# The second MLP product of a decoder layer, by Strassen's scheme for 24 of its 32 feature blocks

## The chip, the cores and the metric

The kernel runs on one NeuronCore of a Trainium2 chip. Five engines work side by side, each through its own queue in order: TensorE (PE) multiplies matrices into PSUM, VectorE (DVE) and ScalarE (ACT) work on SBUF and PSUM elementwise, GpSimd (POOL) on SBUF only, and SyncE (SP) issues transfers. Transfers can be issued from SP, ACT and POOL, and run on 16 DMA engines. The metric is the device time of one execution in microseconds (us).

## The reference

One layer on x of shape 512 x 1024 in float32: an input LayerNorm, a token mixer (gated linear attention beside multi-head latent attention), a LayerNorm over the residual, then the MLP and a last LayerNorm. The change touches the MLP alone:

```python
h = layer_norm(x, ln_in_g, ln_in_b)
mix = token_mixer(h, ...)
h = layer_norm(DEEPNORM_ALPHA * h + mix, ln1_g[l], ln1_b[l])
ff = jnp.square(jax.nn.relu(h @ w_ff1[l])) @ w_ff2[l]
h = layer_norm(DEEPNORM_ALPHA * h + ff, ln2_g[l], ln2_b[l])
```

`w_ff1` is 1024 x 4096 and `w_ff2` 4096 x 1024, all float32. The hidden width 4096 is 32 feature blocks of 128.

## The kernel before

**Precision.** Each float32 operand is held as two float32r parts: hi is the value copied by ACT into the float32r type, lo the rest, which DVE subtracts (`split`, and the same two instructions in `pump`). A product of two operands is three matmuls, hi x hi, hi x lo and lo x hi, added in one PSUM bank.

**The stream of weights.** All weight tiles of the whole kernel stand in one list, `stream`, in the order of their use. `plan` appends tiles of two row blocks by up to 512 columns. `pump(i)` runs ahead of tile i: it issues the loads from SP into `wraw` (three slots) two tiles ahead (`DMA_AHEAD`), and the split into `whi` and `wlo` (two slots each) one tile ahead (`SPLIT_AHEAD`). Tiles marked `res` get slots of their own in pool `pa` and may be split one further ahead.

**The products.** `gemm_fm` computes a product with features on the partitions: weights are stationary, 512 tokens move, and up to four PSUM banks are open. `gemm_tm` computes with tokens on the partitions: the activations are stationary (four tiles of 128 tokens), 512 weight columns move.

**The MLP.** It runs in chunks of 12, 12 and 8 feature blocks (`FC`, L321). For each chunk, the first product is computed with `gemm_fm` in groups of four blocks. `ev_h` (L1047) empties each bank: ACT relu, ACT square into hi of `hid`, POOL the full square, DVE the rest lo. The second product of a chunk then goes through `gemm_tm` for each half of the 1024 output columns, and `ev_res` (L980) adds each bank onto the residual tile `res` with DVE. For the last chunk the second product is ordered by token tiles, so that the last LayerNorm (`ln2`) and the stores can begin early.

**SBUF and PSUM.** Pool `pa` has a group A of 24 slots and a group C of 8 (`TAG_C`), 4 KB of each partition a slot; pool `pb` has 22 slots of 2 KB, of which the normalised input of the MLP, `h1T`, holds 16 until the last first product. The pools `pm` and `px` have four PSUM banks each.

**The order.** The program is written as generators that are stepped between matmuls (`spawn`, `tick`, `finish`). The framework then orders the instructions of each engine at build time, by the order in which they were written and by a simulated timeline, hands out the slots, and places the semaphores. `issue_after` asks for a place behind a given instruction.

Of the kernel before, what the change touches and what calls it, by code (L numbers as in the profile page):

```python
# [52 lines left out]
def tile_hybrid_block(ctx: ExitStack, tc: tile.TileContext, I, out, dbg=None):  # L53
    nc = tc.nc
    dbg = dbg or {}
    consts = ctx.enter_context(tc.tile_pool(name="consts", bufs=1))
    wp = ctx.enter_context(tc.tile_pool(name="wp", bufs=3))
    pa = ctx.enter_context(tc.tile_pool(name="pa", bufs=32))
    pb = ctx.enter_context(tc.tile_pool(name="pb", bufs=22))
    sm = ctx.enter_context(tc.tile_pool(name="sm", bufs=4))  # L60
# [5 lines left out]
    def nm(s):  # L66
        uid[0] += 1
        return f"{s}_{uid[0]}"

    TAG_C = ('h0', 'qn', 'PT1', 'res', 'bc', 'hid1')  # L70

    def A(shape, dt=F32, n="a"):
        return pa.tile(shape, dt, tag="C" if n in TAG_C else "A", bufs=8 if n in TAG_C else 24, name=nm(n))

    def B(shape, dt=F32, n="b"):
        return pb.tile(shape, dt, tag="B", name=nm(n))
# [26 lines left out]
    def split(src, hi, lo, scale=None):  # L103
        if scale is None:
            act(hi, src, AF.Copy)
            return vtt(lo, src, f(hi), op=ALU.subtract)
# [27 lines left out]
    st = {"dma": 0, "spl": 0, "gates": ()}  # L134
    DMA_AHEAD, SPLIT_AHEAD = 2, 1

    def plan(name, c0, n, k_lo=0, k_hi=None, heads=None, res=False):
        w = I[name]
        K = w.shape[0] // P
        k_hi = K if k_hi is None else k_hi  # L140
        idx = []
        for k0 in range(k_lo, k_hi, 2):
            nk = min(2, k_hi - k0)
# [10 lines left out]
        return {"idx": idx, "nk": k_hi - k_lo}  # L154

    def pump(i):
        while st["dma"] < min(len(stream), i + 1 + DMA_AHEAD):
            e = stream[st["dma"]]
            raw = wp.tile([P, 2, T], F32, tag="wraw", name=nm("wraw"))
            for sl, src, cw in e["dmas"]:  # L160
                dst = raw[:, sl, :e["n"]]
                if cw is not None:
                    dst = dst.rearrange("p (h c) -> p h c", c=cw)
                nc.sync.dma_start(dst, src)
            e["raw"] = raw
            st["dma"] += 1
        while st["spl"] < min(len(stream), i + 2 + SPLIT_AHEAD):
            e = stream[st["spl"]]
            if st["spl"] > i + SPLIT_AHEAD and not e["res"]:
                break  # L170
            nk, n = e["nk"], e["n"]
            if e["res"]:
                hi, lo = A([P, 2, T], F32R, "whr"), A([P, 2, T], F32R, "wlr")
            else:
                hi = wp.tile([P, 2, T], F32R, tag="whi", bufs=2, name=nm("whi"))
                lo = wp.tile([P, 2, T], F32R, tag="wlo", bufs=2, name=nm("wlo"))
            raw = e.pop("raw")
            with ExitStack() as gates:
                for g in st["gates"]:
                    gates.enter_context(tc.issue_after(g.ins))  # L180
                st["ins"] = act(hi[:, :nk, :n], raw[:, :nk, :n], AF.Copy)  # L181
                vtt(lo[:, :nk, :n], raw[:, :nk, :n], f(hi[:, :nk, :n]), op=ALU.subtract)  # L182
            st["gates"] = ()
            e["w"] = (hi, lo)
            st["spl"] += 1

    def weights(pl, k):
        i = pl["idx"][k // 2]
        pump(i)
        hi, lo = stream[i]["w"]  # L190
        return hi[:, k % 2, :], lo[:, k % 2, :]


    active = []
# [1 line left out]
    def spawn(g):  # L196
        active.append(g)
        return g
# [22 lines left out]
    def gemm_fm(pl, xs, n, evac, width=None, toks=slice(0, T), accs=None, guard=None):  # L221
        na = n // P
        accs = accs or [MM() for _ in range(na)]
        for k in range(pl["nk"]):
            hi, lo = weights(pl, k)
            xh, xl = part(xs[k], 0, toks), part(xs[k], 1, toks)
            first, last = k == 0, k == pl["nk"] - 1
            for a in range(na):
                c = slice(a * P, (a + 1) * P)
                o = accs[a][:, toks]  # L230
                mm(o, hi[:, c], xh, start=first, stop=False)  # L231
                mm(o, hi[:, c], xl, start=False, stop=False)  # L232
                mm(o, lo[:, c], xh, start=False, stop=last)  # L233
# [77 lines left out]
        PL["ym", mb] = plan("w_o_mla", mb * T, T)  # L311

    def plan_zip(key, specs):
        pls = [{"idx": [], "nk": 8} for _ in specs]
        for k0 in range(0, 8, 2):
            for j, (name, c0, kb, res) in enumerate(specs):
                pls[j]["idx"] += plan(name, c0, T, kb + k0, kb + k0 + 2, res=res)["idx"]
        PL[key] = pls

    plan_zip("out", [("w_out", 0, 0, True), ("w_out", T, 0, True)])  # L320
    FC = (12, 12, 8)  # L321
    fb = 0
    for ci, nb in enumerate(FC):
        for b in range(nb // 4):
            PL["f1", ci, b] = plan("w_ff1", (fb + 4 * b) * P, T, res=(ci == 0 and b == 0))
        if ci < 2:
            for nh in range(2):
                PL["f2", ci, nh] = plan("w_ff2", nh * T, T, fb, fb + nb)
# [651 lines left out]
    def ev_res(a, j, ps):  # L980
        vtt(res[a][:, j * T:(j + 1) * T], ps, res[a][:, j * T:(j + 1) * T], op=ALU.add)
# [59 lines left out]
            nc.sync.dma_start(out[tt * P:(tt + 1) * P, c], r[:, c])  # L1041
        yield

    for ci, nb in enumerate(FC):
        hid = []

        def ev_h(a, ps):  # L1047
            hh = A([P, 2, T], F32R, "hid0" if len(hid) < 8 else "hid1")
            r = B([P, T], F32, "relu")
            act(r, ps, AF.Relu)  # L1050
            act(hh[:, 0, :], r, AF.Square)  # L1051
            gtt(r, r, r, op=ALU.mult)  # L1052
            vtt(hh[:, 1, :], r, f(hh[:, 0, :]), op=ALU.subtract)  # L1053
            hid.append(hh)
        for b in range(nb // 4):
            if ci == 0 and b == 0:
                gemm_fm(PL["f1", ci, b], h1T, T, ev_h, toks=slice(256, T), accs=accs)
                t_r1 = spawn(residual1())
            else:
                gemm_fm(PL["f1", ci, b], h1T, T, ev_h)  # L1060
        if ci == 0:
            finish(t_r1)
        if ci < 2:
            for nh in range(2):
# [71 lines left out]
```

## Time and profile before

| | |
|---|---|
| median of three runs | 918.5 us (918.45 to 918.63) |
| the profiled execution | 918.58 us, its span 916.8 us |
| PE busy | 900.1 us, 98% of the span, 4580 matmuls |
| DVE, ACT, POOL busy | 55%, 38%, 16% |
| first matmul on `hid` | 626.5 us |
| mean granted TensorE clock | 0.998 |

The span runs from the first to the last instruction. Busy shares are means over stages with different limits. Matmuls overlap in the pipeline, so the distance between their starts, not their duration, says what one costs. The rows show engine, line of the kernel, operation, the names of what is written and read, shapes, and a count.

### The profile page before, as it was taken

The page shows a single profiled execution, that of the slowest core. Times are in us where ns is not written, and L with a number is a line of the kernel's source. Part 1 is how long each engine was busy: PE and PEld are TensorE (multiplying, and loading weights), DVE is VectorE, ACT ScalarE, POOL GpSimd, SP SyncE. Part 2 cuts the span into 40 slices and gives each one's busy share as a digit, 9 for nine tenths or more (in the row PEclk, how much of TensorE's full clock was granted, in tenths as well). Part 3 has the DMA queues.
Part 4 walks back from the last instruction along what each step waited for, and adds up shares of the span by engine and source line. Part 5 has one row for each costly group of instructions (what it writes and reads, how often), then busy time and mean ns, then how long its engine had stood idle before and what let it go on. Part 6 is the DMA issues. An engine that isn't in the chain of part 4 may idle for free.

```text
span 916.8 us, 11652 instructions
## 1 busy us (share of the span) xinstructions
PE 900.1 (98%) x4580; PEld 764.8 (83%) x4580; DVE 503.7 (55%) x819; ACT 351.8 (38%) x605; POOL 142.3 (16%) x144
## 2 busy tenths in 40 slices
PE   6999999999999999999999999999999999999996
PEld 5988888888888888888888889988888888888886
DVE  7725864675625245557766877944323444332576
ACT  6464553534434343345545322333121343213410
POOL 1012543352511010000000000322000222001201
PEclk9999999999999999999999999999999999999999
DMA  7313212222213223122217432033222332242312
GB/s 242 116 46 96 88 51 88 70 69 70 58 52 115 64 81 121 29 64 70 75 55 267 139 116 69 10 106 100 106 92 92 94 108 97 92 138 92 116 70 91
DMA packets 52199, 85.22 MB, mean 93 GB/s; under 512 B 6784, under 2 KB 16384, under 8 KB 52144
## 3 DMA queue, kind: packets, MB, share of 16 engines
q1 hardware_dynamic: 50224, 80.82, 27.4%
q10 hardware_dynamic: 1920, 3.66, 1.2%
q8 instruction: 36, 0.59, 0.3%
q14 instruction: 19, 0.16, 0.0%
HBM read 82.36 MB, written 2.10 MB: 92 GB/s over the span
## 4 chain that ended last, share of the span: by engine, by line
PE 97%; ACT 1%; POOL 1%; DVE 1%; DMA 1%; issue 0%; SPq 0%; DVEq 0%
PE mm L231 15%; PE mm L233 15%; PE mm L232 15%; PE mm L264 12%; PE mm L266 12%; PE mm L265 12%; PE px L668 2%; PE px L825 1%; PE px L355 1%; PE px L264 1%; PE px L266 1%; PE px L265 1%; PE px L801 1%; PE px L802 1%; PE px L651 1%; PE px L803 1%
## 5 line engine op out<-in xcount | busy, mean ns | idle before, releaser
L182 DVE TENSOR_TENSOR wlo<-wraw,whi 128x1024 fp32r<-128x1024 f32 (+2 forms) x128 | 147.0, 1149 | 245.3 <-ACT whi L181 236.9
L181 ACT ACTIVATE whi<-wraw 128x1024 fp32r<-128x1024 f32 (+2 forms) x128 | 125.8, 983 | 279.9 <-PE mm L232 134.6
L231 PE MATMUL mm<-h,whi 128*128 128x512 f32 x416 | 162.7, 392 | 0.4 <-ACT gt L912 0.4
L232 PE MATMUL mm<-h,whi 128*128 128x512 f32 x416 | 162.4, 390 | 0.0
L233 PE MATMUL mm<-h,wlo 128*128 128x512 f32 x416 | 151.9, 390 | 0.0
L231 PEld LDWEIGHTS mm<-h,whi 128*128 128x128 f32 x416 | 78.1, 188 | 16.3 <-ACT gt L912 0.6
L233 PEld LDWEIGHTS mm<-h,wlo 128*128 128x128 f32 x416 | 77.9, 188 | 16.3 <-DVE wlo L182 0.3
L232 PEld LDWEIGHTS mm<-h,whi 128*128 128x128 f32 x416 | 78.1, 188 | 15.7
L1052 POOL TENSOR_TENSOR relu<-relu 128x512 f32<-128x512 f32 x32 | 44.0, 1396 | 262.8 <-ACT hid L1051 262.8
L265 PE MATMUL mm<-wlo,hid 128*128 128x512 f32 x192 | 74.7, 389 | 0.0
L266 PE MATMUL mm<-whi,hid 128*128 128x512 f32 x192 | 74.7, 389 | 0.0
L264 PE MATMUL mm<-whi,hid 128*128 128x512 f32 x192 | 65.0, 389 | 0.0
L1053 DVE TENSOR_TENSOR hid<-relu,hid 128x512 fp32r<-128x512 f32 x32 | 40.7, 1311 | 34.2 <-POOL relu L1052 34.2
L265 PE MATMUL mm<-wlo,h 128*128 128x512 f32 x128 | 50.3, 393 | 0.0
L266 PE MATMUL mm<-whi,h 128*128 128x512 f32 x128 | 50.1, 392 | 0.0
L264 PE MATMUL mm<-whi,h 128*128 128x512 f32 x128 | 49.7, 403 | 0.0
L266 PEld LDWEIGHTS mm<-whi,hid 128*128 128x128 f32 x192 | 36.1, 188 | 7.5
L265 PEld LDWEIGHTS mm<-wlo,hid 128*128 128x128 f32 x192 | 36.0, 188 | 7.5
L264 PEld LDWEIGHTS mm<-whi,hid 128*128 128x128 f32 x192 | 36.0, 188 | 7.4
L181 ACT ACTIVATE whr<-wraw 128x1024 fp32r<-128x1024 f32 (+1 forms) x28 | 27.4, 988 | 35.7 <-PE mm L266 16.2
L607 POOL TENSOR_TENSOR rp<-rp 128x256 f32<-128x256 f32 x32 | 31.4, 983 | 60.9 <-ACT E L612 44.1
L340 POOL TENSOR_TENSOR mv<-mv,mhalf 128x1 f32<-128x1 f32 x4 | 2.9, 735 | 225.2 <-DVE mv L339 225.2
(285 smaller groups left out, 1831.7 us busy)
## 6 DMA issues: line engine op xcount, KB each, us to landing
wraw<-in_w_ff_dram SPq DMA_DIRECT2D x64, 512.0 KB, 3.5
wraw<-in_w_in_dram SPq DMA_DIRECT2D x40, 512.0 KB, 3.5
wraw<-in_w_o_gla_dram SPq DMA_DIRECT2D x8, 512.0 KB, 3.7
wraw<-in_w_o_mla_dram SPq DMA_DIRECT2D x8, 512.0 KB, 3.5
wraw<-in_w_out_dram SPq DMA_DIRECT2D x8, 512.0 KB, 3.8
wraw<-in_w_in_dram SPq DMA_DIRECT2D x8, 360.0 KB, 5.0
wraw<-in_w_q_b_dram SPq DMA_DIRECT2D x18, 128.0 KB, 2.2
wraw<-in_w_kv_b_dram SPq DMA_DIRECT2D x16, 128.0 KB, 2.2
```

Of the source, the lines that this page charges most:

```text
L181: st["ins"] = act(hi[:, :nk, :n], raw[:, :nk, :n], AF.Copy)
L182: vtt(lo[:, :nk, :n], raw[:, :nk, :n], f(hi[:, :nk, :n]), op=ALU.subtract)
L231: mm(o, hi[:, c], xh, start=first, stop=False)
L232: mm(o, hi[:, c], xl, start=False, stop=False)
L233: mm(o, lo[:, c], xh, start=False, stop=last)
L264: mm(o, xh, hi[:, :n], start=opens, stop=False, skip_group_check=share)
L265: mm(o, xh, lo[:, :n], start=False, stop=False, skip_group_check=share)
L266: mm(o, xl, hi[:, :n], start=False, stop=last, skip_group_check=share)
L607: gtt(Rv[:, :, 0, :], Rv[:, :, 0, :], Pv[:, :, 1, s - 1:s].to_broadcast([P, n, s]), op=ALU.add)
L668: mm(p[:rows(s), tt * 64:(tt + 1) * 64].rearrange("p (n s) -> p n s", s=s), M[:, tt * P:tt * P + rows(s)], pairs(M[:, c], s)[:, :, 1, :], ...
L1052: gtt(r, r, r, op=ALU.mult)
L1053: vtt(hh[:, 1, :], r, f(hh[:, 0, :]), op=ALU.subtract)
```

## The change

The MLP runs in four chunks of 8 feature blocks. In the first three, the second product of a chunk, 512 tokens x 1024 features by 1024 features x 1024 columns, is cut in two in each direction: tokens 0 to 255 and 256 to 511, even and odd feature blocks, columns 0 to 511 and 512 to 1023. The four blocks of activations are called a11, a12, a21 and a22, those of the weights 11, 12, 21 and 22. Strassen's scheme in Winograd's form then needs seven block products with sums of blocks:

- `win_load` loads the four weight blocks, in two halves each, from POOL's queue: eight transfers of 512 KB per chunk.
- `win_sums` makes T1, T2 and T3 on DVE; T4 is made in `win_f2`. These and the plain blocks are split by `pump` as before, but two tiles ahead; their hi and lo parts lie in slots named by `HOMES`: the usual ones (w), two slots of `wraw` (r), or group A (a).
- `ev_h` keeps a squared pair of feature blocks in float32 (R). `win_hid` makes the four sums of activation blocks on DVE and splits them; a11, a12 and a22 are split as they are. POOL's square is no longer used there.
- `win_f2` runs 14 weight tiles (seven products, two halves) of 12 matmuls. Products that are added share a bank, whose state is taken at the points where it is one of the sums of the scheme: ACT copies the bank to a tile `ev` in pool `pb`, and POOL issues one or two accumulating transfers of 256 KB that add it onto `res`: 16 per chunk.
- The first product of these chunks is computed in groups of two feature blocks with weight tiles of four row blocks by 256 columns (but the very first group, of four blocks).

The last chunk is as before. `hid1` is gone, and the pool `wp` is merged into `pa` with the same numbers of slots.

```diff
-    wp = ctx.enter_context(tc.tile_pool(name="wp", bufs=3))
...
-    TAG_C = ('h0', 'qn', 'PT1', 'res', 'bc', 'hid1')
+    TAG_C = ('h0', 'qn', 'PT1', 'res', 'bc', 'T1', 'T2')
+    TAG_W = {'wraw': 3, 'whi': 2, 'wlo': 2}
...
     def pump(i):
         while st["dma"] < min(len(stream), i + 1 + DMA_AHEAD):
             e = stream[st["dma"]]
-            raw = wp.tile([P, 2, T], F32, tag="wraw", name=nm("wraw"))
+            st["dma"] += 1
+            if "src" in e:
+                continue
+            raw = A([P, e["nk"], T * 2 // e["nk"]], F32, "wraw")
...
-            if st["spl"] > i + SPLIT_AHEAD and not e["res"]:
+            if st["spl"] > i + e.get("ahead", SPLIT_AHEAD) and not e["res"]:
                 break
             nk, n = e["nk"], e["n"]
...
+            hi, lo = [A([P, nk, T * 2 // nk], F32R, w) for w in HOME["a" if e["res"] else e.get("home", "w")]]
+            raw = e["src"]() if "src" in e else e.pop("raw")
...
-    FC = (12, 12, 8)
+    FC = 4
+    F1 = [((0, 4), (4, 2), (6, 2))] + [tuple((b, 2) for b in range(0, 8, 2))] * 2 + [((0, 4), (4, 4))]
+    HOMES = "wwrawarawawawa"
+    HOME = {"w": ("whi", "wlo"), "r": ("wraw", "wraw"), "a": ("xh", "xl")}
+    WIN = (("11", 0, 0), ("21", 0, 1), ("11", 1, 0), ("21", 1, 1), ("T1", 0, 2), ("T1", 1, 2), ("T2", 0, 3), ("T2", 1, 3),
+           ("T4", 0, 4), ("T4", 1, 4), ("22", 0, 5), ("22", 1, 5), ("T3", 0, 6), ("T3", 1, 6))
...
+            PL["f2", ci] = []
+            for n, (op, hf, _) in enumerate(WIN):
+                PL["f2", ci].append(len(stream))
+                stream.append({"src": lambda q=(ci, op, hf): WQ[q], "nk": 2, "n": T, "res": False,
+                               "ahead": 2, "home": HOMES[n]})
...
+    def win_load(ci):
+        w2 = I["w_ff2"].rearrange("(k p) n -> p k n", p=P)
+        for op, i, j in (("12", 0, 1), ("11", 0, 0), ("22", 1, 1), ("21", 1, 0)):
+            for hf in range(2):
+                t = A([P, 2, T], F32, "wq")
+                k0 = 8 * ci + 4 * hf + i
+                nc.gpsimd.dma_start(t, w2[:, k0:k0 + 3:2, j * T:(j + 1) * T])
+                WQ[ci, op, hf] = t
+
+    def win_sums(ci):
+        def held(*a, **kw):
+            with ExitStack() as gates:
+                if "ev" in st:
+                    gates.enter_context(tc.issue_after(st["ev"].ins))
+                vtt(*a, **kw)
+        for hf in range(2):
+            q12 = WQ.pop((ci, "12", hf))
+            t1 = WQ[ci, "T1", hf] = A([P, 2, T], F32, "T1")
+            held(t1, q12, WQ[ci, "11", hf], op=ALU.subtract)
+            yield
+            held(q12, WQ[ci, "22", hf], q12, op=ALU.subtract)
+            WQ[ci, "T3", hf] = q12
+            yield
+            t2 = WQ[ci, "T2", hf] = A([P, 2, T], F32, "T2")
+            held(t2, q12, WQ[ci, "11", hf], op=ALU.add)
+            yield
+
+    def win_hid(R, ops):
+        a11, a12, a21, a22 = R[:, 0, :256], R[:, 1, :256], R[:, 0, 256:], R[:, 1, 256:]
+        X = A([P, 4, 256], F32, "hx")
+        vtt(X[:, 0], a21, a22, op=ALU.add)
+        vtt(X[:, 1], X[:, 0], a11, op=ALU.subtract)
+        yield
+        vtt(X[:, 2], a12, X[:, 1], op=ALU.subtract)
+        vtt(X[:, 3], a11, a21, op=ALU.subtract)
+        yield
+        xh, xl = A([P, 4, 256], F32R, "xh"), A([P, 4, 256], F32R, "xl")
+        split(X, xh, xl)
+        yield
+        t = B([P, 2, 256], F32R, "a22")
+        split(a22, t[:, 0], t[:, 1])
+        ops[2], ops[3], ops[5], ops[6] = [(xh[:, i], xl[:, i]) for i in range(4)]
+        ops[4] = (t[:, 0], t[:, 1])
+        yield
+
+    def win_f2(ci, hid):
+        bank = {}
+        for n, (op, hf, ph) in enumerate(WIN):
+            i = PL["f2", ci][n]
+            pump(i)
+            hi, lo = stream[i]["w"]
+            for pp in range(2):
+                for t in range(2):
+                    key = ({3: 0, 6: 0, 5: 2}.get(ph, ph), t)
+                    opens = key not in bank
+                    if opens:
+                        bank[key] = (PX if key[0] < 2 else MM)()
+                    o, c = bank[key], slice(t * P, (t + 1) * P)
+                    while ph not in hid[2 * hf + pp]:
+                        tick(4)
+                    xh, xl = hid[2 * hf + pp][ph]
+                    mm(o, xh[:, c], hi[:, pp], start=opens, stop=False, skip_group_check=True)
+                    mm(o, xh[:, c], lo[:, pp], start=False, stop=False, skip_group_check=True)
+                    mm(o, xl[:, c], hi[:, pp], start=False, stop=hf == 1 and pp == 1, skip_group_check=True)
+                tick(4)
+            if n in (5, 6):
+                t2, q21 = WT.pop((ci, n - 5))
+                vtt(t2, t2, q21, op=ALU.subtract)
+                WQ[ci, "T4", n - 5] = t2
+            if hf == 1:
+                for t in range(2):
+                    o = bank[{3: 0, 6: 0, 5: 2}.get(ph, ph), t]
+                    e = B([P, T], F32, "ev")
+                    st["ev"] = act(e, o, AF.Copy, scale=-1.0 if ph == 4 else 1.0)
+                    for tt, j in (((0, 0),), ((0, 0),), ((2, 1),), ((0, 1),), ((2, 0),), ((0, 1),), ((2, 0), (2, 1)))[ph]:
+                        nc.gpsimd.dma_start(res[tt + t][:, j * T:(j + 1) * T], e, accum_op=ALU.add)
+            if n == 9 and ci + 1 < FC - 1:
+                win_load(ci + 1)
...
         def ev_h(a, ps):
-            hh = A([P, 2, T], F32R, "hid0" if len(hid) < 8 else "hid1")
             r = B([P, T], F32, "relu")
             act(r, ps, AF.Relu)
+            if win:
+                if a % 2 == 0:
+                    hid.append({"R": A([P, 2, T], F32, "hr")})
+                ops = hid[-1]
+                R = ops["R"]
+                act(R[:, a % 2, :], r, AF.Square)
+                if a % 2:
+                    h1 = A([P, 2, 2, 256], F32R, "h1p")
+                    split(R[:, :, :256], h1[:, 0], h1[:, 1])
+                    ops[0], ops[1] = [(h1[:, 0, i], h1[:, 1, i]) for i in range(2)]
+                    spawn(win_hid(R, ops))
+                return
...
+                gemm_fm(PL["f1", ci, b], h1T, w * P, ev_h, width=2)
+            if win and b == 0:
+                t_ws = spawn(win_sums(ci))
...
-        if ci < 2:
-            for nh in range(2):
-                gemm_tm([PL["f2", ci, nh]], hid, T, lambda a, j, ps: ev_res(a, nh, ps))
+        if win:
+            finish(t_ws)
+            for hf in range(2):
+                WT[ci, hf] = (WQ[ci, "T2", hf], WQ[ci, "21", hf])
+            win_f2(ci, hid)
```

More of the change, by code (lines that the diff above doesn't have):

```diff
@@ L68, in nm @@
         return f"{s}_{uid[0]}"
-    TAG_C = ('h0', 'qn', 'PT1', 'res', 'bc', 'hid1')
+    TAG_C = ('h0', 'qn', 'PT1', 'res', 'bc', 'T1', 'T2')
+    TAG_W = {'wraw': 3, 'whi': 2, 'wlo': 2}
     def A(shape, dt=F32, n="a"):
-        return pa.tile(shape, dt, tag="C" if n in TAG_C else "A", bufs=8 if n in TAG_C else 24, name=nm(n))
+        tag, bufs = ("C", 8) if n in TAG_C else (n, TAG_W[n]) if n in TAG_W else ("A", 24)
+        return pa.tile(shape, dt, tag=tag, bufs=bufs, name=nm(n))
     def B(shape, dt=F32, n="b"):
@@ L135, in tile_hybrid_block, with plan @@
     DMA_AHEAD, SPLIT_AHEAD = 2, 1
-    def plan(name, c0, n, k_lo=0, k_hi=None, heads=None, res=False):
+    def plan(name, c0, n, k_lo=0, k_hi=None, heads=None, res=False, per=2):
         w = I[name]
@@ L141, in plan @@
         idx = []
-        for k0 in range(k_lo, k_hi, 2):
-            nk = min(2, k_hi - k0)
+        for k0 in range(k_lo, k_hi, per):
+            nk = min(per, k_hi - k0)
             if heads is None:
@@ L153, in plan @@
             stream.append({"dmas": dmas, "nk": nk, "n": n, "res": res})
-        return {"idx": idx, "nk": k_hi - k_lo}
+        return {"idx": idx, "nk": k_hi - k_lo, "per": per}
     def pump(i):
@@ L165, in pump @@
             e["raw"] = raw
-            st["dma"] += 1
         while st["spl"] < min(len(stream), i + 2 + SPLIT_AHEAD):
             e = stream[st["spl"]]
-            if st["spl"] > i + SPLIT_AHEAD and not e["res"]:
+            if st["spl"] > i + e.get("ahead", SPLIT_AHEAD) and not e["res"]:
                 break
             nk, n = e["nk"], e["n"]
[L172 to L177, printed above, removed]
+            hi, lo = [A([P, nk, T * 2 // nk], F32R, w) for w in HOME["a" if e["res"] else e.get("home", "w")]]
+            raw = e["src"]() if "src" in e else e.pop("raw")
             with ExitStack() as gates:
@@ L187, in weights @@
     def weights(pl, k):
-        i = pl["idx"][k // 2]
+        per = pl["per"]
+        i = pl["idx"][k // per]
         pump(i)
         hi, lo = stream[i]["w"]
-        return hi[:, k % 2, :], lo[:, k % 2, :]
+        return hi[:, k % per, :], lo[:, k % per, :]
     active = []
@@ L313, in plan_zip @@
     def plan_zip(key, specs):
-        pls = [{"idx": [], "nk": 8} for _ in specs]
+        pls = [{"idx": [], "nk": 8, "per": 2} for _ in specs]
         for k0 in range(0, 8, 2):
@@ L320, in tile_hybrid_block @@
     plan_zip("out", [("w_out", 0, 0, True), ("w_out", T, 0, True)])
-    FC = (12, 12, 8)
-    fb = 0
-    for ci, nb in enumerate(FC):
-        for b in range(nb // 4):
-            PL["f1", ci, b] = plan("w_ff1", (fb + 4 * b) * P, T, res=(ci == 0 and b == 0))
-        if ci < 2:
-            for nh in range(2):
-                PL["f2", ci, nh] = plan("w_ff2", nh * T, T, fb, fb + nb)
+    FC = 4
[4 more added lines that the diff above has]
+           ("T4", 0, 4), ("T4", 1, 4), ("22", 0, 5), ("22", 1, 5), ("T3", 0, 6), ("T3", 1, 6))
+    fb = 0
+    for ci in range(FC):
+        nb = 8
+        for b, w in F1[ci]:
+            PL["f1", ci, b] = plan("w_ff1", (fb + b) * P, w * P, res=(ci == 0 and b == 0), per=8 // w)
+        if ci < FC - 1:
+            PL["f2", ci] = []
[3 more added lines that the diff above has]
+                               "ahead": 2, "home": HOMES[n]})
         else:
@@ L1042, in ln2 @@
         yield
-    for ci, nb in enumerate(FC):
+    def win_load(ci):
[23 more added lines that the diff above has]
+            yield
@@ L1045, in tile_hybrid_block @@
+    WQ, WT = {}, {}
+    for ci in range(FC):
+        nb = 8
         hid = []
+        win = ci < FC - 1
+        if ci == 0:
+            win_load(0)
         def ev_h(a, ps):
-            hh = A([P, 2, T], F32R, "hid0" if len(hid) < 8 else "hid1")
             r = B([P, T], F32, "relu")
             act(r, ps, AF.Relu)
+            if win:
[10 more added lines that the diff above has]
+                return
+            hh = A([P, 2, T], F32R, "hid0")
@@ L1054, in ev_h @@
             hid.append(hh)
-        for b in range(nb // 4):
+        for b, w in F1[ci]:
             if ci == 0 and b == 0:
@@ L1059, in tile_hybrid_block @@
             else:
-                gemm_fm(PL["f1", ci, b], h1T, T, ev_h)
+                gemm_fm(PL["f1", ci, b], h1T, w * P, ev_h, width=2)
+            if win and b == 0:
+                t_ws = spawn(win_sums(ci))
         if ci == 0:
             finish(t_r1)
-        if ci < 2:
-            for nh in range(2):
-                gemm_tm([PL["f2", ci, nh]], hid, T, lambda a, j, ps: ev_res(a, nh, ps))
+        if win:
[3 more added lines that the diff above has]
+            win_f2(ci, hid)
         else:
```

## The prediction

> **What bounds the kernel now.** I read the page first: busy shares, slices and the chain that ended last.
>
> ```profile
> span 916.8 us, 11652 instructions
> PE 900.1 (98%) x4580; PEld 764.8 (83%) x4580; DVE 503.7 (55%) x819; ACT 351.8 (38%) x605; POOL 142.3 (16%) x144
> PE   6999999999999999999999999999999999999996
> DVE  7725864675625245557766877944323444332576
> PEclk9999999999999999999999999999999999999999
> PE 97%; ACT 1%; POOL 1%; DVE 1%; DMA 1%; issue 0%; SPq 0%; DVEq 0%
> ```
>
> TensorE (PE) is busy in every slice at full granted clock, and the chain runs through it for 97% of its length. A matmul taken away is therefore time taken away, as long as nothing makes PE wait. A busy share is no price, because matmuls overlap. The price is the distance between starts, so next come the matmuls of the second MLP product (all that read hid in the first two chunks) and two starts from the timeline with only such matmuls between them:
>
> ```profile
> L264 PE MATMUL mm<-whi,hid x192: 388/389/390, 626.5 to 821.7; 128*128 128x512 f32 x192
> L265 PE MATMUL mm<-wlo,hid x192: 389/389/390, 626.7 to 821.9; 128*128 128x512 f32 x192
> L266 PE MATMUL mm<-whi,hid x192: 389/389/390, 627.0 to 822.1; 128*128 128x512 f32 x192
> ...
> 678.18 0.39 PE L264 MATMUL mm<-whi,hid 128*128 128x512 f32 x1
> ...
> 680.90 1.07 PE L264 MATMUL mm<-whi,hid 128*128 128x512 f32 x4
> ```
>
> The duration is 0.389 us, but from 678.18 to 680.90 twelve matmuls start: 2.72 / 12 = 0.2267 us each. By the duration the gain would come out 1.7 times too large.
>
> Then the stages (columns: window, length, busy PE, PEld, DVE, ACT, POOL, clock, DMA share, GB/s):
>
> ```profile
> 573.00:583.00 10.00, 10.00 (x86) 10.00 (x85) 9.97 (x17) 2.05 (x4) 0.00 (x0) 1.00 0.00 0
> 583.00:605.00 22.00, 22.00 (x100) 18.20 (x99) 12.48 (x11) 8.42 (x14) 8.14 (x5) 1.00 0.23 72
> 605.00:626.50 21.50, 21.50 (x96) 17.81 (x95) 9.83 (x8) 8.06 (x13) 4.94 (x4) 1.00 0.29 99
> 626.50:681.00 54.50, 54.50 (x242) 45.14 (x241) 19.91 (x18) 13.05 (x16) 5.16 (x4) 1.00 0.29 97
> ```
>
> In the second product (626.5 to 681) DVE works 37% and ACT 24% of the time, and PE never waits. The one tight place is 573 to 583, where DVE is full.
>
> **Matmuls removed.** The three rows hold 3 x 192 = 576 matmuls for 24 feature blocks. Strassen's seven products of 4 blocks x 2 token tiles x 3 terms make 7 x 24 = 168 matmuls of the same shape per chunk of 8 blocks, 504 in three chunks. 72 x 0.2267 = 16.3 us go. The first product keeps its count: groups of two feature blocks with four row blocks per weight tile hold the same 24 matmuls as groups of four with two. No transposes are added. The two pools of SBUF are merged with the same slots for wraw, whi and wlo, so the stages before the MLP keep their work.
>
> **Work added to ACT and DVE.** The prices are these rows:
>
> ```profile
> L182 DVE TENSOR_TENSOR wlo<-wraw,whi 128x1024 fp32r<-128x1024 f32 x108 | 134.8, 1249 | 216.0 <-ACT whi L181 209.6 <-PE px L825 3.4 <-PE mm L231 1.4
> L181 ACT ACTIVATE whi<-wraw 128x1024 fp32r<-128x1024 f32 x108 | 114.5, 1060 | 251.2 <-PE mm L266 118.8 <-PE mm L232 114.2 <-issue 8.6
> L363 DVE TENSOR_TENSOR h<-lnt,h 128x256 fp32r<-128x256 f32 x32 | 12.5, 413 | 0.2
> L981 DVE TENSOR_TENSOR res<-mm,res 128x512 f32<-128x512 f32 x26 | 17.7, 688 | 10.1 <-PE mm L266 10.1
> L105 ACT ACTIVATE mv<-mm 128x256 fp32r<-128x256 f32 x16 | 5.6, 380 | 3.0 <-DVE mv L106 2.9
> L1050 ACT ACTIVATE relu<-mm 128x512 f32<-128x512 f32 x32 | 18.9, 596 | 28.6 <-PE mm L233 28.0
> L1051 ACT ACTIVATE hid<-relu x32: 623/637/654, 583.0 to 868.7; 128x512 fp32r<-128x512 f32 x32
> L1053 DVE TENSOR_TENSOR hid<-relu,hid x32: 678/1522/1526, 587.8 to 873.6; 128x512 fp32r<-128x512 f32 x32
> ```
>
> Per chunk, DVE: 8 splits of w_ff1 and 14 of the second product at 1.25 = 27.5; 8 sums of weight blocks at about 1.25 = 10.0; for each of four pairs of feature blocks 0.69 (h1p) + 4 x 0.41 (sums) + 1.25 (split) + 0.41 (a22) = 4.0, so 16.0. Together 53.5 us. ACT: 22 splits x 1.06 = 23.3; four pairs at 2 x (0.60 + 0.64) + 0.64 + 1.06 + 0.38 = 4.6, so 18.3; 14 evictions x 0.60 = 8.4. Together 50.0 us. A chunk lasts (192 + 168) x 0.2267 = 81.6 us. Both fit on average (66% and 61%), so PE remains the bound, and what can be lost is lost at places.
>
> L1053 takes 0.68 us at best and 1.52 while POOL multiplies beside it. 24 of those 32 POOL products go, with the 0.84 us that each can cost DVE. The Trainium skill, "SBUF — State Buffer", section on who interferes with whom, says that a DVE instruction with two SBUF inputs contends with a GpSimd instruction that reads SBUF; this trace agrees.
>
> **Place 1, DVE in the first chunk.** The residual's eight sums end at 586.9, after a gap of 4 us in which nothing was ready:
>
> ```profile
> 570.01 0.99 DVE L362 TENSOR_SCALAR lnt<-px,cb 128x256 f32<-128x256 f32 x2 [4.01 <-ACT h L358]
> ...
> 578.86 3.49 DVE L1022 TENSOR_TENSOR res<-res,bc 128x1024 f32<-128x1024 f32 x3
> 582.27 4.62 DVE L1023 TENSOR_TENSOR res<-res,bc 128x1024 f32<-128x1024 f32 x4
> ```
>
> The first product of the new first chunk ends where 8 blocks are done, at about 605. From 586.9 that is 18.1 us for pairs 0 to 2 (12.0), six weight sums (7.5), two splits of w_ff1 and the first of the second product (3.8): 23.3 us, 5.2 too many. Before, the second product began only at 626.5, after 12 blocks. Now, if DVE takes its work in that order, the first product starts up to 5.2 late. If it takes the urgent splits first, the lack moves to the fifth weight tile (the first that needs a sum), 4 x 2.72 = 10.9 us on, with four splits and pair 3 added: 23.3 + 9.0 = 32.3 for 29.0, 3.3 late. The sums may also move into the gap at 566 to 570. Bounds: 0 to 8 (both lacks). I take 2.5.
>
> **Place 2, the last pair at the end of each first product.** It is needed in the third weight tile's second half, 2.5 x 2.72 = 6.8 us after PE's last matmul of the first product. The old end of that stage shows the queue (PE's last such matmul, then ACT):
>
> ```profile
> 626.28 0.39 PE L233 MATMUL mm<-h,wlo 128*128 128x512 f32 x1
> ```
> ```profile
> 624.72 1.28 ACT L1050 ACTIVATE relu<-mm 128x512 f32<-128x512 f32 x2 [2.63 <-PE mm L233]
> 625.90 0.62 ACT L1051 ACTIVATE hid<-relu 128x512 fp32r<-128x512 f32 x1
> ...
> 627.42 1.06 ACT L181 ACTIVATE whi<-wraw 128x1024 fp32r<-128x1024 f32 x1
> ```
>
> From the last bank on: relu 0.60, square 0.64, one split that stands between 1.06, h1p on ACT 0.64 and DVE 0.69 = 3.6; with a second split on ACT and another DVE instruction ahead, 3.6 + 1.06 + 1.25 = 5.9. That fits with 0.9 us over, less than one DVE instruction. Bounds 0 to 2, three times; I take 0.5 each, 1.5.
>
> **Place 3, evictions and accumulating transfers.** The seven products are no longer added by DVE from PSUM (L981). ACT copies each bank to a tile ev, and POOL issues 48 transfers of 256 KB that add it onto res; each must wait for the earlier one onto the same half row. POOL also issues 24 loads of 512 KB that SP issued before. The trace has no accumulating transfer and none from POOL. The nearest rows (KB each, us to landing):
>
> ```profile
> out_dram<-res SPq DMA_DIRECT2D x8, 256.0 KB, 2.0
> wraw<-in_w_ff_dram SPq DMA_DIRECT2D x64, 512.0 KB, 3.5
> bc<-in_ln_in_b_dram ACTq DMA_DIRECT2D x1, 512.0 KB, 8.5
> ```
>
> ev comes from pool pb, which has 22 slots: 16 hold h1T, 4 the a22 tiles until product five is done, so 2 are free. Product pairs of banks end 3, 4, 6, 8 and 10 weight tiles after the start, u = 2.72 us each. With R from eviction to free slot, product two's eviction waits until 3u + R, product four's until 3u + 3R against 8u: it is 3R - 13.6 late. ACT is blocked behind it, and the next split is wanted within 2u (the look-ahead) less the split's 1.06 + 1.25, so 3.1 us are covered. PE loses 3R - 16.7 per chunk, which is nothing up to R = 5.6. Bounds of R: 0.60 + 2.0 = 2.6 and 0.60 + 8.5 = 9.1. An addition reads its target too, so I take the 512 KB row: 0.60 + 3.5, with 0.5 for POOL's issue, 4.6. Loss 0; I put 0.5 for an ACT instruction that comes late.
>
> The Trainium skill, "DMA: Bandwidth & Descriptors", section "Anatomy of one DMA — SWDGE (gpsimd) path", gives 2.0 us + bytes / 436,000 per us for a transfer issued from POOL: an estimate of 2.6 us for 256 KB, R = 3.2 and no loss; no row here shows such a transfer. Against the change speaks its section "Two DMAs through the same engine are not ordered", with the rule that a second addition to the same bytes waits for the first one's semaphore.
>
> The 24 loads (4 MB per chunk) are issued some four weight tiles before a chunk ends and needed by the sums within the 43.5 us of the next first product; while an addition waits at the head of POOL's queue, they wait behind it. At the 512 KB row, one after the other, 8 x 3.5 = 28 us. They are hidden, with 15 us of cover to spare; late by more than that, they hold up the sums and then PE, us for us.
>
> **The sum.** The profiled execution took 918.58 us: span 916.8 and 1.8 around it. 918.6 - 16.3 + 2.5 + 1.5 + 0.5 = 906.8. The median of the runs is 918.5, 0.1 less, so I say 907.
>
> **Rivals.**
> Slower: place 3 decides. From R = 6.9 on, the loss of 3 x (3R - 16.7) = 12.0 eats the 11.8 that are left of the gain. At R = 8 it is 21.9 us: 906.8 + 21.9 = 929 us. For it: the 8.5 us row, the two free slots, ACT's strict order, loads in the same POOL queue. Against it: the 2.0 us row of the same size. Chance 0.17.
> DVE becomes the bound at place 1 with its full 8 us, and place 2 with 2 us each: 918.6 - 16.3 + 8 + 6 + 0.5 = 917; for it the 9.97 of 10.00 us, against it the 37% in the later product. Between 912 and 917: chance 0.13; of this 0.05 ends within 0.2% of no change.
> The full gain, every place hidden: 902.3, as PE's wait-free stages now suggest. Chance of under 904: 0.15.
> It doesn't do what it says (a matmul costs more with the new tiles, so nothing is saved): shape and operands' types are those of the rows above. Chance 0.03, 918, counted as no change.
>
> **How the numbers follow.** 904 to 912, the forecast's own range: 0.52. Under 904: 0.15. 912 to 916.7: 0.08. Within 0.2% (916.7 to 920.3, what a measurement of this kernel can't tell from no change): 0.08. Slower: 0.17. So faster 0.75. The range runs from 902, all hidden, to 922, which leaves out about 0.13 above (R past 7.3) and 0.03 below.
>
> **What would show it.** Right: 72 fewer PE matmuls; starts still 0.2267 apart; weight-sum and pair instructions on DVE between 587 and 605, with a PE wait of a few us on DVE near 605 to 618 and none over 1 us at the later two starts; accumulating transfers landing within 4 us. Wrong: ev on ACT waiting for a transfer by more than 3 us while PE waits for whi (the slower rival); a PE wait over 5 us at the first start (DVE); PE waiting for wq, that is for loads; or a changed span before 557 us, where I expect none.

## The result, and the profile after

The changed kernel takes 903.12 us (median of 4 runs, 902.52 to 903.90), the kernel before 918.57 us (918.45 to 919.26): a ratio of 0.9831, 95% interval 0.9814 to 0.9848, so 15.5 us or 1.7% faster. The profiled execution took 902.75 us with a span of 901.0, 15.8 less than the span before.

From the page of the changed kernel, the busy times and the chain that ended last:

```profile
span 901.0 us, 11740 instructions
PE 883.8 (98%) x4508; PEld 751.3 (83%) x4508; DVE 553.4 (61%) x905; ACT 412.7 (46%) x701; POOL 170.1 (19%) x192
PE 97%; ACT 1%; POOL 1%; DVE 1%; DMA 1%; issue 0%; SPq 0%; DVEq 0%
```

72 PE matmuls are gone (4580 to 4508), PE's busy time fell by 16.3 us (900.1 to 883.8), and the chain still runs through PE for 97%. DVE has 50 us more to do and ACT 61, and neither shows in the chain. The whole list of what PE waited for between 540 and 890 us (us in total, times, longest) is one line:

```profile
PE mm L231 <- ACT h L369: 0.3, 1, 0.3
```

It is a wait of the first product's first matmuls for the LayerNorm's output. From there to the end of the MLP PE waits for nothing. The stages that were shown of before, in the same windows:

```profile
573.00:583.00 10.00, 10.00 (x86) 10.00 (x86) 9.97 (x17) 1.68 (x4) 0.00 (x0) 1.00 0.00 0
583.00:605.00 22.00, 22.00 (x101) 18.27 (x100) 21.33 (x31) 14.60 (x25) 0.00 (x0) 1.00 0.01 1
605.00:626.50 21.50, 21.50 (x97) 17.80 (x96) 18.53 (x20) 15.54 (x21) 5.68 (x8) 1.00 0.36 84
626.50:681.00 54.50, 54.50 (x242) 45.15 (x241) 30.08 (x38) 29.03 (x43) 14.21 (x18) 1.00 0.74 199
```

DVE (the third busy column) is 97% busy or more from 573 to 605 and 86% after, yet PE (the first) fills every window. The transfers of the page (KB each, median us to landing):

```profile
wraw<-in_w_ff_dram SPq DMA_DIRECT2D x40, 512.0 KB, 4.5
wq<-in_w_ff_dram POOLq DMA_DIRECT2D x24, 512.0 KB, 8.8
res<-ev POOLq DMA_DIRECT2D x48, 256.0 KB, 6.6
```

An accumulating transfer lands after 6.6 us, more than the 3.5 that the prediction took. So the gain came nearly whole, although place 3 looked worse than predicted. The experiments ask where the gain comes from, and why places 1 and 3 cost nothing.

Each experiment's ratio is to the kernel before, timed beside it; multiplied by 918.57 it gives the second time below, by which experiments are compared. Its interval is mostly about 1.4 us to either side.

### The profile page after: what moved, and what is told of

It reads as the page before. It is cut to its first block, busy times and chain, and to the rows that moved or that the text cites. A ratio compares the mean times of both kernels' runs of the same rounds, so it can differ in the third digit from the quotient of the medians.

```text
span 901.0 us, 11740 instructions
## 1 busy us (share of the span) xinstructions
PE 883.8 (98%) x4508; PEld 751.3 (83%) x4508; DVE 553.4 (61%) x905; ACT 412.7 (46%) x701; POOL 170.1 (19%) x192
## 4 chain that ended last, share of the span: by engine, by line
PE 97%; ACT 1%; POOL 1%; DVE 1%; DMA 1%; issue 0%; SPq 0%; DVEq 0%
PE mm L231 16%; PE mm L233 15%; PE mm L232 15%; PE mm L264 7%; PE mm L266 7%; PE mm L265 7%; PE px L1116 2%; PE px L1118 2%; PE px L1117 2%; PE mm L1116 2%; PE mm L1118 2%; PE mm L1117 2%; PE px L679 2%; PE px L836 1%; PE px L366 1%; PE px L264 1%
## 5 line engine op out<-in xcount | busy, mean ns | idle before, releaser
L181 DVE TENSOR_TENSOR wlo<-wraw,whi 128x1024 fp32r<-128x1024 f32 (+1 forms) x104 | 117.7, 1133 | 169.6 <-ACT whi L180 162.2
L180 ACT ACTIVATE whi<-wraw 128x1024 fp32r<-128x1024 f32 (+1 forms) x104 | 100.3, 964 | 134.1 <-PE mm L232 82.4
L231 PEld LDWEIGHTS mm<-h,whi 128*128 128x128 f32 x416 | 78.1, 188 | 16.3 <-ACT gt L923 0.6
L232 PEld LDWEIGHTS mm<-h,whi 128*128 128x128 f32 x416 | 78.1, 188 | 15.7
L1130 POOL DMA_DIRECT2D res<-ev x48 | 42.2, 1042 | 188.9 <-ACT ev L1128 151.5
L180 ACT ACTIVATE xh<-wraw 128x1024 fp32r<-128x1024 f32 (+1 forms) x28 | 27.3, 986 | 34.8 <-PE mm L266 16.1
L618 POOL TENSOR_TENSOR rp<-rp 128x256 f32<-128x256 f32 x32 | 31.5, 984 | 60.8 <-ACT E L623 44.0
L625 DVE TENSOR_TENSOR M<-E,qk 128x512 f32<-128x512 f32 x32 | 27.3, 854 | 16.5 <-ACT E L623 16.5
L181 DVE TENSOR_TENSOR xl<-wraw,xh 128x1024 fp32r<-128x1024 f32 (+1 forms) x28 | 31.1, 1126 | 8.0 <-ACT xh L180 8.0
L623 ACT ACTIVATE E<-rp 128x512 f32<-128x512 f32 x32 | 20.4, 638 | 26.9 <-POOL rp L619 26.9
L619 POOL TENSOR_TENSOR rp<-rp 128x256 f32<-128x256 f32 x32 | 27.6, 862 | 10.3 <-ACT q L648 8.1
L266 PEld LDWEIGHTS mm<-whi,h 128*128 128x128 f32 x128 | 24.1, 188 | 5.0
L265 PEld LDWEIGHTS mm<-wlo,h 128*128 128x128 f32 x128 | 24.1, 188 | 4.3
```

Source lines behind the costliest of these rows:

```text
L265: mm(o, xh, lo[:, :n], start=False, stop=False, skip_group_check=share)
L266: mm(o, xl, hi[:, :n], start=False, stop=last, skip_group_check=share)
L1130: nc.gpsimd.dma_start(res[tt + t][:, j * T:(j + 1) * T], e, accum_op=ALU.add)
```

## The experiments

### Where the gain comes from

**The four chunks without Strassen.** All second products are plain, in the changed kernel's chunks and groups; the plan of weight tiles follows, and the loads of weight blocks go.

```diff
-        win = ci < FC - 1
+        win = ci < 0
...
+        elif ci < FC - 1:
+            for nh in range(2):
+                gemm_tm([PL["f2", ci, nh]], hid, T, lambda a, j, ps: ev_res(a, nh, ps))
```

> The changed kernel's four chunks of eight feature blocks and its groups of two, but the second product of all chunks plain as before (eight block products, DVE adds the banks, POOL squares), no Strassen. Theory count (the gain is 72 matmuls at 0.2267 us and nothing else): 918.5 us, within 1 us of the kernel before. Rival (the smaller chunks and groups bring part of the gain by themselves): 904 to 914 us.

Measured: 918.85 us, ratio 0.9995 (0.9986 to 1.0004). The page has the old number of matmuls:

```profile
PE 900.2 (98%) x4580; PEld 764.7 (83%) x4580; DVE 506.0 (55%) x827; ACT 351.2 (38%) x605; POOL 137.2 (15%) x144
```

Chunks and groups alone bring nothing. The gain is that of the matmuls.

**Strassen in two chunks of three.** The same edit with `win = ci < 2`.

> The changed kernel with Strassen's scheme in the first two chunks alone and a plain second product in the third. Theory count: 24 matmuls come back, 24 x 0.2267 = 5.4 us: 908.5 us. Rival (the gain is not proportional, since the chunks differ in what they wait for): 904 to 906 or over 911 us.

Measured: 909.00 us, ratio 0.9887 (0.9872 to 0.9902), that is 908.2 us: 5.1 us back for 24 matmuls, where 5.4 were expected. The gain goes with the count.

**DVE adds the bank states.** The part of the change that is new in kind is left out.

```diff
-                    e = B([P, T], F32, "ev")
-                    st["ev"] = act(e, o, AF.Copy, scale=-1.0 if ph == 4 else 1.0)
...
-                        nc.gpsimd.dma_start(res[tt + t][:, j * T:(j + 1) * T], e, accum_op=ALU.add)
+                        rr = res[tt + t][:, j * T:(j + 1) * T]
+                        if ph == 4:
+                            st["ev"] = vtt(rr, rr, o, op=ALU.subtract)
+                        else:
+                            st["ev"] = vtt(rr, o, rr, op=ALU.add)
```

> The changed kernel, with the bank states added onto the residual by DVE straight from PSUM (16 additions of 0.69 us per chunk) in place of ACT's copies and the accumulating transfers. ACT loses 8.4 us of work per chunk, DVE gains 11.0 us to 64.5 of 81.6 us. Theory count (whatever fits behind PE costs nothing): 902 to 905 us, the same as with the transfers. Rival (DVE is too full near the ends of the first products, and the transfers are what saves the gain): 908 us or more, with PE waiting for DVE.

Measured: 903.32 us, ratio 0.9825 (0.9810 to 0.9839). DVE's busy share rises from 61% to 65%, and PE again waits 0.3 us in all. The accumulating transfers contribute nothing that can be measured; the same gain is to be had without them and without their risk, which the next group shows.

### Why late evictions cost nothing

How long the additions took to land in the changed kernel, in three windows: around the second products of chunk one (600 to 660), two (660 to 750) and three (760 to 830), in this order. Only the third has no loads of a next chunk's weight blocks beside it.

```profile
res<-ev POOLq DMA_DIRECT2D x16, 256.0 KB, 9.4
...
res<-ev POOLq DMA_DIRECT2D x16, 256.0 KB, 9.8
...
res<-ev POOLq DMA_DIRECT2D x16, 256.0 KB, 4.7
```

With R = 0.6 + 9.4 the prediction's formula gives a loss of 3 x 10.0 - 16.7 = 13 us in the first two chunks. But these are medians of all 16 additions of a chunk, and the formula concerns the first ones. The first four landed in 4.3 to 5.5 us in chunk one and in 3.3 to 6.0 in chunk two; the late ones were issued after the loads. Still, ACT did wait for slots of ev (us in total, times, longest):

```profile
ACT ev L1128 <- DMA res<-ev: 30.2, 17, 4.7
```

The timeline of ACT shows why PE noticed none of it:

```profile
597.98 1.04 ACT L180 ACTIVATE wraw<-T 128x1024 fp32r<-128x1024 f32 x1
...
615.97 1.09 ACT L1128 ACTIVATE ev<-px 128x512 f32<-128x512 f32 x2 [0.78 <-PE px L1118]
618.18 1.06 ACT L180 ACTIVATE whi<-T 128x1024 fp32r<-128x1024 f32 x1 [1.12 <-DVE T L1122]
619.15 1.05 ACT L180 ACTIVATE whi<-wq 128x1024 fp32r<-128x1024 f32 x1
621.32 0.60 ACT L1128 ACTIVATE ev<-px 128x512 f32<-128x512 f32 x1 [1.12 <-DMA res<-ev]
622.66 0.60 ACT L1128 ACTIVATE ev<-px 128x512 f32<-128x512 f32 x1 [0.74 <-DMA res<-ev]
623.16 1.05 ACT L180 ACTIVATE xh<-T 128x1024 fp32r<-128x1024 f32 x1
624.10 1.05 ACT L180 ACTIVATE xh<-wq 128x1024 fp32r<-128x1024 f32 x1
627.56 0.60 ACT L1128 ACTIVATE ev<-mm 128x512 f32<-128x512 f32 x1 [2.40 <-DMA res<-ev]
629.13 0.60 ACT L1128 ACTIVATE ev<-mm 128x512 f32<-128x512 f32 x1 [0.97 <-DMA res<-ev]
...
630.58 1.07 ACT L1128 ACTIVATE ev<-px 128x512 f32<-128x512 f32 x2
```

Splits stand between the evictions, earlier than the code puts them. By the slots they write, those at 619.15 and 624.10 make the eleventh and twelfth weight tile (the two halves of block 22), which PE reaches 10 and 11 x 2.72 us after 605.1, at 632.3 and 635.0. They are 13 and 11 us ahead; the other splits behind an eviction are 6 to 11 us ahead, not at most 5.4. T2's first split, at 597.98, came before any eviction and 21 us before its use at 619.17.

The evictions were also less late than the formula has it. The two free slots came back after 5.3 to 6.5 us (615.97 to 621.32 and 627.56; the second of the pair to 622.66 and 629.13). Product four's eviction, at 630.58, waited for no transfer. Both slots had just been taken, but PE had finished the first two a22 tiles at 629.8. In the second chunk the trace names a matmul on a22 as the end of three of ACT's waits for ev, so the a22 slots come back one by one during product five, and not after it.

**Splits held behind the evictions.** The splits run no further ahead than the prediction assumed.

```diff
                 for g in st["gates"]:
                     gates.enter_context(tc.issue_after(g.ins))
+                if "src" in e and "ev" in st:
+                    gates.enter_context(tc.issue_after(st["ev"].ins))
```

> The changed kernel, with each weight split of the second products on ACT put behind the latest eviction ev written before it, so that the splits can run ahead of PE by two weight tiles and no further past a waiting eviction, as the prediction assumed. Theory look-ahead (the prediction's delay 3R - 13.6 is real, but the order on ACT lets the splits run 8 us or more ahead, and that covered it): with R = 0.6 + 9.4 us beside the loads of the next chunk and 0.6 + 4.7 in the third chunk, the loss is 3 x 10.0 - 16.7 = 13 us in each of two chunks and none in the third: 903 + 26 = 929 us. Rival (late evictions block nothing that PE needs): 903 to 905 us.

Measured: 913.33 us, ratio 0.9937 (0.9921 to 0.9954), that is 912.8 us: 9.7 of the 15.5 us are lost. ACT in the first chunk, then PE at the same time:

```profile
616.71 1.09 ACT L1130 ACTIVATE ev<-px 128x512 f32<-128x512 f32 x2 [2.58 <-PE px L1120]
617.68 1.06 ACT L182 ACTIVATE xh<-T 128x1024 fp32r<-128x1024 f32 x1
622.06 0.60 ACT L1130 ACTIVATE ev<-px 128x512 f32<-128x512 f32 x1 [3.33 <-DMA res<-ev]
623.38 0.60 ACT L1130 ACTIVATE ev<-px 128x512 f32<-128x512 f32 x1 [0.72 <-DMA res<-ev]
623.88 1.05 ACT L182 ACTIVATE wraw<-T 128x1024 fp32r<-128x1024 f32 x1
```
```profile
624.98 0.73 PE L1118 MATMUL px<-wraw,xh 128*128 128x512 f32 x2 [2.37 <-ACT wraw L182]
626.24 0.50 PE L1119 MATMUL px<-wraw,xh 128*128 128x512 f32 x1 [0.52 <-DVE wraw L183]
...
627.37 0.63 PE L1120 MATMUL px<-wraw,xl 128*128 128x512 f32 x1
627.80 0.63 PE L1118 MATMUL px<-wraw,xh 128*128 128x512 f32 x1
```

The eviction of product two waits for product one's transfer, the split of T2 stands behind it, and PE waits 2.9 us. After the wait matmuls start 0.43 us apart for some 3 us. By the starts of the same matmuls in both traces, the first chunk loses 5.4 us. The same chain, with shorter waits, costs 1.8 us in each of the other two. So the loss comes in all three chunks, the third too, and not at product four with 13 us in two, as expected. The first round trip alone decides (616.7 to 622.1, 5.3 us); after it PE itself is late, and from 632 us on the evictions wait for PE and not for a slot. So the theory of the look-ahead held, but not its place nor its size: 9.7 where 26 was expected.

**The control: the same order, with DVE adding ev.**

```diff
-                        nc.gpsimd.dma_start(res[tt + t][:, j * T:(j + 1) * T], e, accum_op=ALU.add)
+                        rr = res[tt + t][:, j * T:(j + 1) * T]
+                        vtt(rr, rr, e, op=ALU.add)
```

> The kernel whose splits stand behind the evictions (913.3 us), with ev added onto the residual by DVE in place of the accumulating transfers, so that a slot of ev comes back after 0.6 + 0.7 us. Theory round trip (the 10 us were lost because the splits stood behind evictions that waited for a transfer of 5 to 6 us): 903 to 905 us. Rival (putting the splits behind the evictions costs by itself): 909 to 914 us.

Measured: 904.25 us, ratio 0.9835 (0.9820 to 0.9849). The order costs nothing by itself (903.4 against 903.1). What cost was the round trip of the transfer with splits queued behind it.

**Every addition in two halves.**

```diff
-                    st["ev"] = act(e, o, AF.Copy, scale=-1.0 if ph == 4 else 1.0)
+                    st["ev"] = act(e, o, AF.Copy, scale=-0.5 if ph == 4 else 0.5)
...
+                        for _ in range(2):
                             nc.gpsimd.dma_start(res[tt + t][:, j * T:(j + 1) * T], e, accum_op=ALU.add)
```

> The changed kernel, with each eviction at half scale and added onto the residual twice, so 96 accumulating transfers in place of 48, the second of each pair waiting for the first. The sum is the same. Round trip R of a free slot about doubled: some 10 us in the third chunk, 18 to 20 us beside loads. Theory look-ahead: 8 to 13 us of cover are not enough any more in the first two chunks, 3 x 18 - 13.6 - 13 = 27 us lost in each at most, less since four more slots come free after product five: 915 to 950 us, with PE waiting for weight splits. Rival (evictions never reach PE): 903 to 905 us.

Measured: 931.91 us, ratio 1.0133 (1.0113 to 1.0154): slower than the kernel before. What PE waited for from 550 us on, the two largest lines:

```profile
PE mm L231 <- ACT ev L1128: 8.5, 3, 4.1
PE mm L1116 <- ACT ev L1128: 7.2, 4, 3.4
```

PE waits for the evictions themselves, 15.7 us in all: it needs a bank that isn't emptied yet. For splits, which the theory named, it waits 4.7 us. So late evictions can make this kernel slower than before, as the slower rival said, but mainly by a path that neither it nor the theory had. From which round trip on they cost time was not measured; it lies between that of the changed kernel and about twice that.

**One free slot in place of two.** `bufs=22` of pool `pb` becomes 21.

> The changed kernel, with 21 in place of 22 slots in pool pb, so that one slot and not two is free for evictions until product five is done. Theory eviction chain (the delay comes from free slots times round trip, and the splits' look-ahead covers some 8 to 13 us of it): each eviction waits for the one before it to land, 6.5 us and more apart, eight of them by product four at 52 us where PE is there at 22 us; PE loses 10 to 25 us per chunk: 930 to 980 us. Rival (slots don't decide, only the DMA engines' load does): 903 to 906 us.

Measured: 906.84 us, ratio 0.9869 (0.9853 to 0.9886), that is 906.5: 3.4 us lost, where 27 or more were expected. PE waits 1.3 us for an eviction. The count of a chain of eight single round trips was wrong. A line of ACT in this run shows it: two evictions go one right after the other at 625.68, when by that count one slot was free. The second line is from the list of who waited for the tiles a22 (us, times):

```profile
625.68 1.09 ACT L1128 ACTIVATE ev<-px 128x512 f32<-128x512 f32 x2 [1.93 <-PE mm L1118]
...
  ACT ev L1128: 2.9, 3
```

So evictions took a22's slots as soon as PE had read them. PE had begun with the tiles a22 at 623.0, in place of 626.9 in the changed kernel: the framework had planned another order of PE's work. How much of the expected loss that order saved is not shown.

**The loads, from SP's queue.** `nc.gpsimd.dma_start` in `win_load` becomes `nc.sync.dma_start`.

> The changed kernel, with the 24 loads of the weight blocks issued from SP in place of POOL, so that accumulating transfers no longer share POOL's queue with them. Theory shared engines (the additions land late, 9.4 us against 4.7 us without loads beside, because the loads fill the 16 DMA engines): additions in the first two chunks still land in 8 to 10 us; time 902 to 904 us. Rival (they wait behind the loads in POOL's own queue): they land in about 5 us; the time is the same, since PE waits for neither.

Measured: 907.24 us, ratio 0.9870 (0.9855 to 0.9885), that is 906.6: 3.5 us lost, which neither theory expected. The additions of the first two chunks land in 7.2 and 7.3 us, between the two forecasts. The loads now share SP's queue with the weights of the next first product. ACT waited for one of those:

```profile
ACT whi L180 <- DMA wraw<-in_w_ff_dram: 6.8, 1, 6.8
```

PE's waits add up to 2.7 us, for splits, 0.7 of them in the first chunk's first product; after the longest ones the clock drops (last section). That SP's order of transfers causes them all is not shown.

**The loads written later.** `if n == 9` before `win_load` becomes `if n == 13`.

> The changed kernel with the loads of the next chunk's weight blocks written after the last weight tile, not after the tenth. Theory shared engines (additions land late beside loads because both share the DMA engines and POOL's queue): additions of the first two chunks land in 4 to 6 us as in the third chunk, in place of 9.4; the loads have 43 us left for 28, the sums come later, and the time is 902.5 to 905 us. Rival (the additions are slow there for another reason): they stay at 8 to 10 us.

Measured: 903.29 us, ratio 0.9823 (0.9807 to 0.9840), and additions at 9.9 and 9.1 us. The experiment says nothing about shared engines, since the loads didn't move. POOL in the changed kernel, then in this run:

```profile
624.13 5.33 POOL L1061 DMA_DIRECT2D wq<-in_w_ff_dram  x7
```
```profile
625.12 4.62 POOL L1061 DMA_DIRECT2D wq<-in_w_ff_dram  x6
```

Wherever they are written, the framework issues them at about the same time; that they go when slots of group A come free is the likely reason, not a shown one. Whether queue or engines make the additions late beside loads stays open.

### Why place 1 cost nothing

The timeline of DVE in the changed kernel has three of the six weight sums at 563.8 to 569.0, in and just before the gap that the prediction named, and one more among the residual's sums. The split of the second product's first weight tile is in time for its start at 605.1:

```profile
563.75 1.21 DVE L1069 TENSOR_TENSOR T<-wq,wq 128x1024 f32<-128x1024 f32 x1
564.99 1.23 DVE L1069 TENSOR_TENSOR wq<-wq,wq 128x1024 f32<-128x1024 f32 x1
...
567.75 1.22 DVE L1069 TENSOR_TENSOR T<-wq,wq 128x1024 f32<-128x1024 f32 x1
...
586.05 1.22 DVE L1069 TENSOR_TENSOR T<-wq,wq 128x1024 f32<-128x1024 f32 x1
...
601.50 1.22 DVE L181 TENSOR_TENSOR wlo<-wq,whi 128x1024 fp32r<-128x1024 f32 x1
```

**The sums behind the LayerNorm.**

```diff
+                if ci == 0:
+                    gates.enter_context(tc.issue_after(st["ln"][1].ins))
                 if "ev" in st:
```

> The changed kernel, with the first chunk's six weight sums put behind the last DVE instruction of the LayerNorm (as the residual's sums are), so that the three that ran at 563 to 569 us can't use that gap. Theory crowding (the gap is what saved the 2.5 us that the prediction put on place 1): 3.6 us of DVE work move behind 577 us, where DVE was busy 21.3 of 22 us until 605 and 18.5 of 21.5 after, and PE waits for DVE by 1 to 3 us near 605 to 618: 904 to 906 us. Rival (the deadlines there leave DVE room; only splits are urgent, sums are not): 902 to 904 us, no PE wait.

Measured: 906.75 us, ratio 0.9861 (0.9846 to 0.9876), that is 905.8: 2.7 us lost. DVE, then PE, then the two windows after the wait:

```profile
595.55 1.22 DVE L1071 TENSOR_TENSOR wq<-wq,wq 128x1024 f32<-128x1024 f32 x1
596.69 1.22 DVE L181 TENSOR_TENSOR wlo<-wraw,whi 128x1024 fp32r<-128x1024 f32 x1
```
```profile
597.96 0.85 PE L233 MATMUL mm<-h,wlo 128*128 128x512 f32 x2 [2.12 <-DVE wlo L181]
```
```profile
597.00:600.00 3.00, 2.04 (x6) 1.59 (x7) 3.00 (x5) 0.25 (x1) 0.00 (x0) 0.74 0.00 0
600.00:603.00 3.00, 3.00 (x11) 2.40 (x10) 2.66 (x4) 1.45 (x2) 0.00 (x0) 0.69 0.00 0
```

The crowding theory holds. PE waits 2.1 us for a split, but at 598 and for the first product's weights, earlier than named. The residual's sums and the weight sums stood ahead of that split in DVE's queue. In this profile PE loses 4.0 us between 583 and 605 (by the starts of the same matmuls), more than it waits; the clock column, after POOL, shows why.

**T1 and T2 of the first chunk computed three times**, as well as late.

> As the kernel with late sums, and T1 and T2 of the first chunk are each computed three times: 8 extra DVE instructions of 1.22 us, 9.8 us, the result unchanged. Theory crowding: DVE is 9.8 + 3.6 us over what it had, 0.7 + 3.0 us of that are idle until 626 us, so PE waits some 5 to 10 us: 908 to 913 us. Rival (place 1 had more room than the prediction gave it): under 906 us.

Measured: 913.75 us, ratio 0.9937 (0.9922 to 0.9952), that is 912.8: 9.7 us lost, 7.0 more than with the late sums alone, for 9.8 us of extra sums. DVE has hardly any room left there: some seven tenths of what it gets beyond goes to PE, in part as lower clock after the waits (5.4 us of them).

## Why the prediction was right

The prediction said 907, in a range from 902 to 922; measured were 903.1. The forecast's way and range held. But the time lies below the forecast's own 904 to 912, and the case that came is the rival "the full gain, every place hidden" (902.3), which had 0.15: the 4.5 us set down for the three places were not lost. The 0.8 us above 902.3 are within the interval.

**The matmuls.** 72 x 0.2267 = 16.3 us was right: PE's busy time fell by 16.3, the span by 15.8, the medians by 15.5. The price by starts and not by the 0.389 us of a row was the step that carried the forecast; plain chunks (0.9995) and two chunks (5.1 us for 24 matmuls) confirm it. The averages of DVE and ACT work were no bound, as said.

**Place 1, 2.5 us: measured 0.** The mechanism was right, the choice of value wrong. The prediction saw that the sums could move into the gap and took half the loss all the same. Late sums cost 2.7 us, close to what was set down, but by luck: the wait was at another split and earlier, and lower clock after it made part of the loss.

**Place 2, 1.5 us: measured 0.** The third and fourth tiles were not waited for. PE's order is planned too: with the fourth tile's operands not yet there (DVE makes the last of them from 614.66 on), PE took T1's product first, from 611.9 on, and the fourth tile from 616.0 on:

```profile
611.92 0.62 PE L1116 MATMUL mm<-whi,xh 128*128 128x512 f32 x2
...
616.00 0.62 PE L1116 MATMUL px<-xh,h1p 128*128 128x512 f32 x2
```

The prediction kept PE's order of the code.

**Place 3, 0.5 us: measured 0, but for another reason than given.** Three terms failed. R was taken as 4.6 from the 512 KB row of a plain load; the round trips that count were 5.3 to 6.5 in the first chunk, and beside loads later additions landed in 9.4 and 9.8 us in the median. "The next split is wanted within 2u (the look-ahead)" was read off the code, where the profile shows splits 6 to 13 us ahead behind the evictions, and T2's first 21. And "4 the a22 tiles until product five is done" was too strict: product four took their slots, so its lateness was 3.5 us (its banks were full at 627.0) and did not grow with R. The last two errors hid the first. Holding the splits behind the evictions brought 9.7 us of loss back, doubling the additions 27.7.

The formula 3R - 16.7 is refuted. With the splits held, a round trip of 5.3 us cost 5.4 us in the first chunk, where it gives none, since the wait came at product two and not four. The break-even R = 6.9 as such was hardly tried: the changed kernel's early round trips lay mostly below it.

The Trainium skill, "DMA: Bandwidth & Descriptors", section "Anatomy of one DMA — SWDGE (gpsimd) path", gave an estimate of 2.6 us for 256 KB. The quickest accumulating transfer took 3.3, the median without loads beside 4.7. What an addition does beyond a copy is not in that fit; which part of it takes the time no run here shows.

**The named signs.** Right: 72 fewer matmuls, distance unchanged, DVE's new work between 587 and 605, PE busy as before until 557. Wrong: no wait near 605 to 618, and additions landing in 6.6 and not within 4 us. Half of the slower rival's sign came, ACT waiting up to 4.7 us for a transfer, but PE did not wait for a split.

## What to carry to other kernels

Price a matmul that is taken away by the distance between starts, and look for the loss only at places where the added work has a deadline. Such a place is judged by the order that the engine's queue really has: here the build moved sums, splits, loads and even matmuls by several us, and the look-ahead of splits that was read off the code was too short, mostly by a factor of up to two and for one split by a factor of four. Before a transfer takes over an addition from an engine with room to spare, try the engine: DVE did it in the same time, without the round trip that made the kernel slower than before once it was doubled.

## What the runs showed of the hardware that was not expected

A wait of PE can cost more than its length. After the waits of 2.37 and 0.52 us in the kernel with splits held back, a window of 3 us has half the granted clock (the column after POOL):

```profile
621.00:624.00 3.00, 1.61 (x8) 0.98 (x6) 0.00 (x0) 1.22 (x3) 0.86 (x1) 1.00 0.60 105
624.00:627.00 3.00, 1.50 (x5) 0.93 (x6) 2.04 (x2) 2.47 (x3) 0.86 (x1) 0.94 0.91 156
627.00:630.00 3.00, 3.00 (x9) 2.33 (x8) 3.00 (x4) 2.03 (x3) 1.73 (x2) 0.50 0.61 104
```

Seven matmuls start in the last 3 us, 0.43 us apart (x9 counts those that run in it), where 13 fit at full clock. The late sums show the same: 2.1 us of waiting, then two windows at 0.74 and 0.69, and a span longer by 4.5 us (905.5 against 901.0). So does the kernel with the loads on SP's queue, after waits of 1.2 and 0.8 us close together:

```profile
640.00:644.00 4.00, 3.19 (x7) 2.34 (x8) 3.97 (x4) 3.84 (x6) 2.39 (x3) 0.64 1.07 372
```

The second chunk's waits of 0.73 and 0.53 us with splits held back left the clock at 1.00, and so did a single one of 1.3 us with one free slot. The Trainium skill, "TensorE: Matmul & The Clock Gate", section "Why this matters for your kernels", warns of idle gaps over about 3 us. Here gaps of 2.1 and 2.4 us were enough, and 2.0 us in two pieces.

Accumulating transfers of 256 KB within SBUF, issued from POOL at 0.87 us each, land in 3.3 us at best, 4.7 in the median with no loads of weight blocks beside, and 9.4 to 9.8 in the two chunks that load 4 MB beside them; a plain store of the same size to DRAM lands in 2.0.
